# Two sides of memory, gate passes ahead of value passes, and the last GLA chain among the merge's first units, in a hybrid attention and GLA decoder step

## The chip, the core and the metric

The kernel runs on one core of one Trainium2 chip. A core has TensorE (PE, matrix multiply), VectorE (DVE), ScalarE (ACT), GpSimd (POOL) and SyncE (SP, which here issues nearly all DMA transfers), all started by their own streams of instructions and ordered among one another by semaphores. The metric is the device time of one execution in microseconds (us).

## What is computed

One decoder layer on 2048 prompt tokens and 8 x 8 sample tokens (2112 rows of 1024 numbers in float32). Cut to what matters:

```python
z = x @ w_in                      # q k v g_att gq gk gv g_gla g_lr r_att r_gla
o_att = sliding_window_attention(q, k, v)          # window 128, sinks, relative bias
o_gla, S = gated_linear_attention(gq, gk, gv, log_a)   # 4 heads, recurrent state S
h_att = (o_att * silu(g_att)) @ w_pa
h_gla = (norm(o_gla) * silu(g_gla)) @ w_pg
merged = sigmoid(r_att) * h_att + sigmoid(r_gla) * h_gla
x = layer_norm(alpha * x + merged @ w_o)
```

Every product of float32 matrices is done as three matmuls on split numbers: a tile is split into a high part (ScalarE, a cast) and a low part (VectorE, the difference), and hi x hi, hi x lo and lo x hi are added in PSUM. That is why each weight and each activation costs a cast on ACT and a subtraction on DVE (`split`, L113 to L115).

## The kernel before, in words

**Stages.** (1) Six chunks of 384, 384, 384, 384, 256 and 320 tokens go through attention (L520 to L622). (2) For each of four heads the same six chunks go through GLA (L832 to L919). (3) The merge multiplies four pairs of matrices (L929 to L1093). (4) The output stage multiplies by w_o and normalizes (L1099 to L1144). Results between the stages go through DRAM: `ua_d` (attention, gated), `ug_d` (GLA, gated), `mg_d` (merged).

**Ticks.** Inside stages 1 and 2 the big projections of a chunk are written in order, and after each stands a `tick()`. Small steps are put into a list by `at(d, fn)`, to be run at the d-th tick. In GLA the steps of a chunk (`gla_a`, `gla_b`, `gla_c`, for each block of 128 tokens, and for the last chunk of a head `samp_a`, `samp_b` for the sample tokens) thus run among the projections of the next chunk. `drain()` runs what is left. The last chunk of the last head has no next chunk: at L929 `drain()` runs its chain by itself, then the pool of buffers is closed and the merge's pool is opened.

For the last chunk of a head (two full blocks and 64 sample tokens) the ticks hold: `gla_a` of the blocks at 0 and 1, `samp_a` at 1 (it makes `kz` and loads two 512-KB state tiles, L779 to L782), `gla_b` of the blocks at 2 and 3, `samp_b(0)` at 3 right behind `gla_b` (its L795 reads both state tiles), `samp_b(4)` at 4. The next head's first chunk writes its first value tile before tick 0 and its second before tick 2.

**Order.** TensorE runs in the order in which the program is written. For the other engines and SP a planner fixes the order when the program is built, by its own estimate of when inputs and buffers are ready, with program order as the priority. On the chip each engine then keeps that order: an instruction that waits holds up those behind it, and so do DMA issues on SP.

**Buffers.** A pool has tags; tiles of a tag share a number of buffers. Tag `w` (28 tiles of 4 KB per partition) holds projection weights (high and low part), the operands of the combinations below, the sample caches kc and vc, and also scores, transposed scores, GLA's ring, states, values, kz and state tiles. A pool opened after another one closed reuses its memory, and each tile waits only for the tiles that lay where it lies.

**The merge.** Each of the four products (w_pa, w_ra, w_pg, w_rg; PA, RA, PG, RG below) is a `Pass` with Winograd's form of Strassen's seven products: `ORDER = (1, 2, 7, 6, 5, 3, 4)` are the operations, s = 0, 1, 2 are three strips of 704 tokens, each cut in two of 352. A unit is one operation on one strip, a group one of its four pairs of output blocks p (`for p in range(NP4)`). Before there are 4 x 7 x 3 = 84 units of 4 groups; a group is 12 matmuls (L1088 to L1090; 6 in PA). `combine` adds products into accumulators `ac` from PSUM; operations 2, 5, 3 and 4 each finish one output block, which goes to the pass's sink.

The passes run PA, RA, PG, RG. PA stores its result in `ha_d`. RA's sink (`sink_ra`, L1055) loads the partner from `ha_d`, takes tanh, forms (tanh + 1) * h (L1058) and stores `ta_d`. PG stores `hg_d`. RG's sink (`sink_rg`, L1061) loads two partners, from `hg_d` and `ta_d`, does the same (L1064), adds on POOL (L1065) and stores `mg_d`. A partner is loaded where the sink is written, with six buffers (tag `cs`).

The differences of the activations that the operations need are made beforehand for x and for the attention result (`combine_x`, L815: 18 combinations, each two loads, four POOL operations and four stores into `xc_d` or `ac_d`, in the first three chunks of heads 0, 1 and 2). For the GLA result (PG) they are made inside the pass on POOL (L1006) from two tiles, kept in `uc_d` and read again. x tiles are loaded one unit ahead (`mv`), weights three units ahead, all four p together (L1082), with differences on POOL (L962 to L973).

**The output stage.** After the merge's pool has closed, a new pool is opened; x tiles are read from `mg_d`, the eight tiles of w_o are loaded and split (through L127), then 17 blocks of rows run.

## Time and profile before

| | us |
|---|---|
| median of 3 runs | 1937.02 |
| lowest and highest run | 1935.22, 1937.87 |
| the profiled execution | 1931.98 |
| its span | 1930.2 |
| TensorE busy in it | 1821.2 (94%) |
| VectorE, ScalarE, POOL busy | 1234.5, 848.1, 504.7 |
| last matmul of GLA's last projection ends | 1078.1 |
| first matmul of the merge | 1103.09 |
| first matmul of the output stage | 1721.38 |

How to read it: the span runs from the first to the last instruction in the trace, and the execution is 1.8 us longer. Times are from the span's start. A row of a timeline has start, duration, engine, line, operation, tiles, and in brackets how long the engine sat idle before it and what ended that. In a row of windows the numbers are the window, its length, busy time and count for each engine (PE, PEld for weight loads, DVE, ACT, POOL; TensorE alone if one line is asked for), then the TensorE clock that was granted, as a share of full speed, the mean busy share of the 16 DMA engines, and GB/s. Matmuls overlap, so the duration of one is longer than the step from one to the next. L114 and L115 are `split`, whoever calls it.

### The profile page before, as it was taken

The numbers are of one execution on the slowest core, as the hardware profiler recorded it, in microseconds if no ns is written. First come the engines' busy times: TensorE is split into PE (matmuls) and PEld (weight loads), VectorE is DVE, ScalarE is ACT, GpSimd is POOL, SyncE is SP. The second block draws the span as 40 slices with busy tenths as digits, with TensorE's granted clock in tenths as the row PEclk, the third lists the DMA queues.
The fourth block names the chain that finished last, engine by engine and source line by source line (L and its number), as shares of the span: only waits on it lengthen the run. The fifth ranks groups of instructions, "written<-read, shape, count | busy, mean of one in ns | idle before, by whom it ended". The sixth has DMA issues, their size and how long they took to land.

```text
span 1930.2 us, 32049 instructions
## 1 busy us (share of the span) xinstructions
PE 1821.2 (94%) x11669; PEld 1728.9 (90%) x11669; DVE 1234.5 (64%) x2544; ACT 848.1 (44%) x1942; POOL 504.7 (26%) x632
## 2 busy tenths in 40 slices
PE   8799999899999999999999799999999989959997
PEld 7688998799999999999999699999989989847886
DVE  5386778655676676567565467678627566756565
ACT  4244446545665565566465343535423333331110
POOL 2410111412133114201101150420544354421121
PEclk9899999999999999999999899999999999969999
DMA  6411013543365246333221479769687765874432
GB/s 199 105 53 37 12 45 98 160 134 113 95 225 182 69 147 221 115 105 113 77 74 48 137 231 321 238 189 323 215 272 268 271 220 169 251 242 166 151 129 81
DMA packets 195038, 304.15 MB, mean 158 GB/s; under 512 B 20648, under 2 KB 162824, under 8 KB 194864
## 3 DMA queue, kind: packets, MB, share of 16 engines
q1 hardware_dynamic: 188960, 294.45, 46.8%
q0 software_dynamic: 5920, 7.66, 1.9%
q8 instruction: 91, 1.49, 0.3%
q14 instruction: 67, 0.55, 0.1%
HBM read 221.19 MB, written 81.81 MB: 157 GB/s over the span
## 4 chain that ended last, share of the span: by engine, by line
PE 72%; DMA 9%; POOL 6%; DVE 5%; issue 4%; ACT 2%; SPq 1%; POOLq 0%; DVEq 0%; ACTq 0%
PE pd L179 9%; PE pd L180 9%; PE pd L181 9%; PE pa L1089 6%; PE pa L1088 6%; PE pa L1090 6%; PE pd L194 6%; PE pd L193 6%; PE pd L192 6%; DMA bs_d<-brow 2%; DMA cs<-hg_d 2%; DMA xs<-ug_d 2%; PE pa L394 1%; DVE wl L115 1%; PE pa L379 1%
## 5 line engine op out<-in xcount | busy, mean ns | idle before, releaser
L179 PE MATMUL pd<-x,wh 128*128 128x384 f32 (+2 forms) x1248 | 409.9, 328 | 17.8 <-ACT x L114 17.1
L180 PE MATMUL pd<-x,wh 128*128 128x384 f32 (+2 forms) x1248 | 404.7, 324 | 3.9 <-DVE x L115 3.9
L181 PE MATMUL pd<-x,wl 128*128 128x384 f32 (+2 forms) x1248 | 404.1, 324 | 1.3 <-DVE wl L115 1.3
L1089 PE MATMUL pa<-xl,wh 128*128 128x352 f32 x1176 | 382.7, 325 | 16.9 <-DVE xl L115 16.5
L1088 PE MATMUL pa<-xh,wh 128*128 128x352 f32 x1176 | 384.2, 327 | 13.6 <-ACT xh L114 9.6
L1090 PE MATMUL pa<-xh,wl 128*128 128x352 f32 x1176 | 381.6, 324 | 0.0
L192 PE MATMUL pd<-wh,x 128*128 128x256 f32 (+1 forms) x768 | 251.6, 328 | 20.5 <-ACT wh L114 20.3
L179 PEld LDWEIGHTS pd<-x,wh 128*128 128x128 f32 x1248 | 237.1, 190 | 27.4 <-ACT x L114 17.7
L194 PE MATMUL pd<-wl,x 128*128 128x256 f32 (+1 forms) x768 | 248.3, 323 | 2.3 <-DVE wl L115 2.2
L193 PE MATMUL pd<-wh,x 128*128 128x256 f32 (+1 forms) x768 | 247.7, 322 | 0.4 <-POOL x L115 0.2
L1089 PEld LDWEIGHTS pa<-xl,wh 128*128 128x128 f32 x1176 | 224.7, 191 | 21.7 <-DVE xl L115 21.7
L180 PEld LDWEIGHTS pd<-x,wh 128*128 128x128 f32 x1248 | 237.2, 190 | 5.6 <-DVE x L115 5.6
L181 PEld LDWEIGHTS pd<-x,wl 128*128 128x128 f32 x1248 | 236.9, 190 | 1.9 <-DVE wl L115 1.9
L1088 PEld LDWEIGHTS pa<-xh,wh 128*128 128x128 f32 x1176 | 223.5, 190 | 16.4 <-ACT xh L114 10.3
L1090 PEld LDWEIGHTS pa<-xh,wl 128*128 128x128 f32 x1176 | 223.5, 190 | 0.0
L115 DVE TENSOR_TENSOR xl<-xs,xh 128x1408 fp32r<-128x1408 f32 (+1 forms) x84 | 130.5, 1553 | 123.2 <-ACT xh L114 108.5
L192 PEld LDWEIGHTS pd<-wh,x 128*128 128x128 f32 x768 | 148.5, 193 | 33.4 <-ACT wh L114 23.9
L114 ACT CAST xh<-xs 128x1408 fp32r<-128x1408 f32 (+1 forms) x84 | 102.8, 1224 | 143.5 <-PE pa L1090 84.1
L194 PEld LDWEIGHTS pd<-wl,x 128*128 128x128 f32 x768 | 148.1, 193 | 16.1 <-DVE wl L115 6.2
L193 PEld LDWEIGHTS pd<-wh,x 128*128 128x128 f32 x768 | 148.3, 193 | 10.8 <-POOL x L115 0.5
L114 ACT CAST x<-xst 128x384 fp32r<-128x384 f32 (+3 forms) x164 | 77.7, 485 | 146.4 <-PE pd L193 123.1
L712 POOL TENSOR_SCALAR sq<-sq 128x1 f32<-128x1 f32 (+1 forms) x68 | 18.8, 277 | 399.4 <-ACT ring L711 399.4
(288 smaller groups left out, 3233.1 us busy)
## 6 DMA issues: line engine op xcount, KB each, us to landing
wst<-wt SPq DMA_DIRECT2D x41, 512.0 KB, 3.6
xs<-ug_d SPq DMA_DIRECT2D x27, 704.0 KB, 6.2
xs<-xc_d SPq DMA_DIRECT2D x24, 704.0 KB, 6.1
u<-xT SPq DMA_DIRECT2D x84, 192.0 KB, 3.7
xst<-xT SPq DMA_DIRECT2D x76, 192.0 KB, 2.7
xs<-xT SPq DMA_DIRECT2D x18, 704.0 KB, 6.2
x<-xT SPq DMA_DIRECT2D x24, 352.0 KB, 5.7
xc_d<-x SPq DMA_DIRECT2D x48, 176.0 KB, 1.8
```

The source lines that it names most:

```text
L114: nc.scalar.copy(dst_h, src)
L115: eng.tensor_tensor(dst_l, src, dst_h.bitcast(F32), ALU.subtract)
L179: mm(ps, hi[:, s], xh[:, :T], start=(k == 0), stop=False)
L180: mm(ps, hi[:, s], xl[:, :T], start=False, stop=False)
L181: mm(ps, lo[:, s], xh[:, :T], start=False, stop=(k == n - 1))
L192: mm(ps, xh[:, xs], hi, start=(k == 0), stop=False)
L193: mm(ps, xl[:, xs], hi, start=False, stop=False)
L194: mm(ps, xh[:, xs], lo, start=False, stop=(k == KT - 1))
L379: nc.tensor.transpose(tp[:, g * P:(g + 1) * P], s[:, g, hf * W:(hf + 1) * W], ident)
L1088: mm(ps, wh[:, ks], xh[:, ts], start=(k == 0), stop=False)
L1089: mm(ps, wh[:, ks], xl[:, ts], start=False, stop=False)
L1090: mm(ps, wl[:, ks], xh[:, ts], start=False, stop=(k == q.kh - 1))
```

## The change

1. **Two sides.** The stages' memory is one pool on the left (`sb`) and one on the right (`sx`). Projection weights, x tiles, combination operands, kc, vc, kcT, vn and p12 go right: tag `xw` has 20 buffers. Scores, GLA's ring, states, values, kz and state tiles stay left: tag `w` has 8. The merge's tiles (`mb`) go right when `sx` closes, so the left pool can stay open for the last GLA chain.
2. **The last chain.** `drain()` no longer stands ahead of the merge. Units call `tick()` after every second group; at unit 6 what is left is drained, the left pool is closed, and pools for partners and `a21` (`ml`) and for combinations (`mc`) are opened there. Until then products use the three `pd` banks of PSUM, afterwards the five `pa` banks.
3. **Order of passes.** RA, PA, RG, PG. The gate passes store tanh in `ta_d` and `tg_d`; the value passes form (tanh + 1) * h, and PG adds `mg_d` of PA on POOL.
4. **U combinations.** Twelve more entries of `combine_x` make the four differences of the GLA result in units 8 to 52, one every four units; PG reads them like x.
5. **Fetching ahead.** x tiles are loaded two units ahead (three buffers) and split one ahead; weights are loaded one step and prepared one step ahead, p by p, spread over the three strips; operation 6 loads two of its blocks again and differences are formed in place. Partners are loaded four groups ahead (eight buffers).
6. **Output weights.** w_o has its own input; five of its eight tiles are loaded and split in units 64 to 80, the rest after the merge.

The diff, cut:

```diff
-        return sb.tile([P, D], dt, tag="w", name=name, bufs=28)
+        return sb.tile([P, D], dt, tag="w", name=name, bufs=8)
+
+    def xwtile(dt=F32, name="xw"):
+        return sx.tile([P, D], dt, tag="xw", name=name, bufs=20)
...
-        kc = wtile(name="kc").rearrange("p (b c) -> p b c", b=NB)
-        vc = wtile(name="vc").rearrange("p (b c) -> p b c", b=NB)
+        kc = xwtile(name="kc").rearrange("p (b c) -> p b c", b=NB)
+        vc = xwtile(name="vc").rearrange("p (b c) -> p b c", b=NB)
...
-                   [(io["xT"], xc_d, 4, k, s) for s in range(MS) for k in range(4)])
+                   [(io["xT"], xc_d, 4, k, s) for s in range(MS) for k in range(4)] +
+                   [(ug_d, uc_d, 4, k, s) for s in range(MS) for k in range(4)])
...
-    drain()
-    phase.close()
...
+    right.close()
+    mb = right.enter_context(tc.tile_pool(name="mb", bufs=1, side="right", reuse_waits="tile"))
...
+        def raw_w(self, i, p):
+            out = []
+            for c, k in {1: [(1, 1)], 2: [(1, 2)], 7: [(1, 1), (2, 1)], 6: [(2, 1), (2, 2), (1, 1)], 5: [],
+                         3: [(1, 2)], 4: [(2, 2)]}[i]:
+                t = mtile("ws", KT // 2 * P, 11)[:, :self.kh * P]
+                nc.sync.dma_start(t, self.w[c - 1, k - 1, p])
+                out.append(t)
+            return out
...
+        def partners(self, i, p, s):
+            if i not in FINAL:
+                return []
+            c, t = FINAL[i]
+            out = []
+            for d in self.parts:
+                y = ml.tile([P, T], F32, tag="cs", name="cs", bufs=8)
+                nc.sync.dma_start(y, d[:, 2 * p + c, toks(s, t)])
+                out.append(y)
+            return out
...
+    def gate_sink(dst):
+        def sink(z, parts, ct, ts):
+            nc.scalar.activation(z, z, AF.Tanh, scale=0.5)
+            nc.sync.dma_start(dst[:, ct, ts], z)
+        return sink
+
+    def merge_sink(z, parts, ct, ts):
+        nc.vector.scalar_tensor_tensor(z, parts[0], 1.0, z, ALU.add, ALU.mult)
+        if len(parts) > 1:
+            nc.gpsimd.tensor_tensor(z, z, parts[1], ALU.add)
+        nc.sync.dma_start(mg_d[:, ct, ts], z)
...
-    passes = [Pass(io["w_pa"], 2, ua_d, store_to(ha_d), ac_d, True),
-              Pass(io["w_ra"], 4, io["xT"], sink_ra, xc_d, True),
-              Pass(io["w_pg"], 4, ug_d, store_to(hg_d), uc_d, False),
-              Pass(io["w_rg"], 4, io["xT"], sink_rg, xc_d, True)]
+    passes = [Pass(io["w_ra"], 4, io["xT"], xc_d, [], gate_sink(ta_d)),
+              Pass(io["w_pa"], 2, ua_d, ac_d, [ta_d], merge_sink),
+              Pass(io["w_rg"], 4, io["xT"], xc_d, [], gate_sink(tg_d)),
+              Pass(io["w_pg"], 4, ug_d, uc_d, [tg_d, mg_d], merge_sink)]
...
     for n, (q, i, s) in enumerate(units):
-        xh, xl = mv
-        if n + 1 < len(units):
-            q2, i2, s2 = units[n + 1]
-            mv = q2.moving(i2, s2)
...
+        if n == 2 * MS:
+
+            drain()
+            left.close()
+            ml = left.enter_context(tc.tile_pool(name="ml", bufs=1, side="left", reuse_waits="tile"))
+            bg = ExitStack()
+            mc = bg.enter_context(tc.tile_pool(name="mc", bufs=1, side="left", reuse_waits="tile"))
+        if n == 3 * len(ORDER) * MS:
+            bg.close()
+            mo = left.enter_context(tc.tile_pool(name="mo", bufs=1, side="left", reuse_waits="tile"))
+        if ml is not None and n < 3 * len(ORDER) * MS and n % 4 == 0 and combos:
+            combine_x(lambda t: mc.tile([P, 2 * T], F32, tag="xc", name=t, bufs=4))
+        if mo is not None and n % 4 == 0 and len(wo) < 5:
+            wo.append(wo_load(mo, len(wo), 10))
+        issue_x(n + 2)
+        issue_w(n + 1)
+        make_x(n + 1)
+        make_w(n)
+        xh, xl = xp.pop(n)
         for p in range(NP4):
...
+            g = n * NP4 + p
+            if ml is not None:
+                for j in range(g, g + 4):
+                    if j not in parts:
+                        issue_parts(j)
...
+            q.combine(i, p, s, ps, parts.get(g))
+            if p % 2:
+                tick()
+    right.close()
```

More of the change, by code (lines that the diff above doesn't have):

```diff
@@ L848 @@
             gla_z(B)
-            if c < 3:
-                combine_x(2)
+            if c < 3 and len(combos) > 12:
+                for _ in range(2):
+                    combine_x(lambda n: xwtile(name=n))
             wv = [wt2("v", 0), wt2("v", 1)]
@@ L1072 @@
[L1072 to L1085 removed]
+                z = acc.pop((p, s, 12))
@@ new lines, in combine @@
+                add(z, z, ps, ALU.add)
+            else:
+                z = acc.pop((p, s, 21))
+                add(z, z, ps, ALU.subtract)
+            if z is not None:
+                c, t = FINAL[i]
+                self.sink(z, parts, 2 * p + c, toks(s, t))
+    def gate_sink(dst):
[8 more added lines that the diff above has]
+        nc.sync.dma_start(mg_d[:, ct, ts], z)
@@ new lines, with issue_w, make_w, issue_x @@
+    raws, wts, xs, xp, parts = {}, {}, {}, {}, {}
+    def issue_w(n):
+        for u, q, i, p in plan.get(n, []):
+            raws[u, p] = q.raw_w(i, p)
+    def make_w(n):
+        for u, q, i, p in plan.get(n, []):
+            wts[u, p] = q.prep_w(i, p, raws.pop((u, p)))
+    def issue_x(n):
+        if n < len(units):
+            q, i, s = units[n]
+            xs[n] = q.raw_x(i, s)
+    def make_x(n):
+        if n < len(units):
+            xp[n] = units[n][0].prep_x(xs.pop(n))
+    def issue_parts(g):
+        if g < len(groups):
+            q, i, s, p = groups[g]
+            parts[g] = q.partners(i, p, s)
@@ new lines, in wo_load @@
+    def wo_load(pool, i, bufs):
+        st = pool.tile([P, D], F32, tag="wst", name="wst", bufs=2)
+        nc.sync.dma_start(st, io["w_o"][i])
+        hi, lo = (pool.tile([P, D], F32R, tag="wo", name=n, bufs=bufs) for n in ("woh", "wol"))
+        split(hi, lo, st)
+        return hi, lo
+    issue_x(0)
+    issue_w(-1)
+    issue_x(1)
+    make_x(0)
+    make_w(-1)
+    issue_w(0)
+    ml = mc = mo = None
+    wo = []
+    for n, (q, i, s) in enumerate(units):
+        if n == 2 * MS:
[16 more added lines that the diff above has]
+        xh, xl = xp.pop(n)
+        for p in range(NP4):
+            g = n * NP4 + p
[3 more added lines that the diff above has]
+                        issue_parts(j)
+            wh, wl = wts[n - s, p]
+            ps = (pd() if ml is None else pa())[:, :T]
@@ L1144 @@
         x = xn
+    right.close()
+    left.close()
 def _consts():
@@ L1200, in _layout @@
         t += [cm(gg[:, h * HV + m * P:h * HV + (m + 1) * P]) for m in range(2)]
[L1201 to L1202 removed]
+    t_o = [rows(wo[:, nh * 512:(nh + 1) * 512], k0) for nh in range(2) for k0 in range(0, KT, 2)]
     def blocks(m):
```

228 lines of the change are left out of this document (80 added, 148 removed).

## The prediction

> **What bounds the kernel now.** I read the page first, then TensorE's waits and timeline, then counts of one matmul line over growing windows, which give the pace of each stage.
>
> ```profile
> span 1930.2 us, 32049 instructions
> PE 1821.2 (94%) x11669; PEld 1728.9 (90%) x11669; DVE 1234.5 (64%) x2544; ACT 848.1 (44%) x1942; POOL 504.7 (26%) x632
> ```
>
> TensorE carries the span, and the change takes no matmul away. So it can win only TensorE's holes, and lose by making new ones. The merge issues 1176 triples (L1088 to L1090). The next rows give window, length, busy time and, in brackets, how many L1090 had been issued by the window's end.
>
> ```profile
> 0.00:1110.00 1110.00, 3.29 (x8) 0.98 0.36 111
> 0.00:1190.00 1190.00, 54.66 (x168) 0.98 0.39 121
> 0.00:1350.00 1350.00, 161.76 (x503) 0.98 0.44 138
> 0.00:1525.00 1525.00, 272.46 (x844) 0.98 0.47 151
> 0.00:1705.00 1705.00, 381.60 (x1176) 0.98 0.50 159
> ```
>
> From 1190 to 1350 pass RA issued 335 triples in 160 us: 0.4776 us each, 7.63 us for a unit of 16. I take this as the full pace, since TensorE shows almost no wait there. PA (168 triples) would need 80.2 us at it, each other pass (336) 160.5. The holes are worst around the merge:
>
> ```profile
> 1077.81 0.31 PE L181 MATMUL pd<-x,wl 128*128 128x320 f32 x1
> 1078.00:1094.40 16.40, 11.26 (x72) 8.36 (x70) 9.90 (x36) 4.68 (x17) 3.52 (x6) 0.90 0.32 105
> 1103.09 0.66 PE L1088 MATMUL pa<-xh,wh 128*128 128x352 f32 x1 [8.76 <-ACT xh L114]
> 1721.38 0.80 PE L192 MATMUL pd<-wh,x 128*128 128x512 f32 x1 [17.09 <-ACT wh L114]
> 1760.00:1800.00 40.00, 40.00 (x178) 33.13 (x177) 25.43 (x37) 6.08 (x12) 6.75 (x8) 1.00 0.44 149
> 1700.00:1918.00 218.00, 102.21 (x256) 0.94 0.47 158
> 1916.95 0.28 PE L208 MATMUL pd<-wh,x 128*128 128x256 f32 x1
> ```
>
> The last projection ends at 1078.1, the last GLA chain runs alone (11.26 us busy of 16.4), and the merge starts at 1103.1: 25 us. With both tables PA took 87 us, RA 160.5, PG 172.5 (to 1523, its 840th triple), RG 181.3: the merge's last matmul ends at 1721.38 - 17.09 = 1704.3, and the output stage starts 17 us later. That stage's pace is 178 matmuls in 40 us, 0.2247 each; 256 triples (the count of L192) are 172.6 us, the 64 half-wide matmuls of the last block some 7.2, and 13.0 pass from the last matmul to the end: 193 us, against 225.9 since 1704.3.
>
> **The change part by part.**
>
> *Start of the merge.* The chain's ticks come every second group of the first units, whose inputs (xT, xc_d) don't wait for GLA. The chain keeps its TensorE work: 11.26 us at clock 0.90, say 10. The first unit still needs x and four weights split into tiles that GLA's last weights may hold; no row shows which. Bounds: 0, and 8.8 (today's wait). I take 3, because freed weight buffers let most loads go before 1078. VectorE and POOL take the chain's small steps between splits; the U differences start only at unit 8. So 25 becomes 13: **-12**.
>
> *Passes RA and RG (gates).* They lose the partner loads and the products. RA has no holes, so what is taken from it wins nothing: 160.5. RG becomes like RA: 161. Fetching two units ahead covers today's waits for x there.
>
> *Pass PA (value).* It gets what RA lost, in half the TensorE time: 48 partner loads and 48 products. VectorE first (count, busy us, mean ns):
>
> ```profile
> L115 DVE TENSOR_TENSOR xl<-xs,xh 128x704 fp32r<-128x704 f32 x21 | 20.8, 990 | 16.1 <-ACT xh L114 16.1
> L115 DVE TENSOR_TENSOR wl<-ws,wh 128x256 fp32r<-128x256 f32 x20 | 9.5, 513 | 0.9 <-ACT wh L114 0.9
> L1032 DVE TENSOR_TENSOR ac<-ac,pa 128x352 f32<-128x352 f32 x12 | 6.1, 511 | 0.0
> L1058 DVE SCALAR_TENSOR_TENSOR ac<-ac,cs 128x352 f32<-128x352 f32 x46 | 26.5, 586 | 4.8 <-ACT ac L1057 3.4 <-DMA cs<-ha_d 0.6
> ```
>
> 21 x 0.99 + 28 x 0.51 + 72 sums x 0.51 + 48 products x 0.59 = 100 us, above TensorE's 80. Now the bytes (KB each, us to landing):
>
> ```profile
> wst<-wt SPq DMA_DIRECT2D x41, 512.0 KB, 3.6
> xs<-xc_d SPq DMA_DIRECT2D x24, 704.0 KB, 6.1
> xc_d<-x SPq DMA_DIRECT2D x48, 176.0 KB, 1.8
> cs<-ha_d SPq DMA_DIRECT2D x48, 176.0 KB, 4.6
> x<-xT SPq DMA_DIRECT2D x24, 352.0 KB, 5.7
> ws<-w_pg SPq DMA_DIRECT2D x28, 256.0 KB, 4.3
> mg_d<-ac SPq DMA_DIRECT2D x48, 176.0 KB, 2.6
> ws<-w_pa SPq DMA_DIRECT2D x28, 128.0 KB, 3.5
> xs<-ua_d SPq DMA_DIRECT2D x9, 352.0 KB, 4.4
> 1160.00:1210.00 50.00, 49.04 (x303) 47.70 (x301) 37.41 (x67) 21.53 (x34) 3.92 (x3) 1.00 0.94 318
> 1630.00:1710.00 80.00, 67.92 (x396) 66.16 (x394) 55.78 (x89) 27.02 (x44) 36.08 (x34) 0.93 0.80 253
> ```
>
> In PA: 21 x tiles 7.6 MB, 36 weights 4.7 (28 before: operation 6 loads two blocks again), 48 partners and 48 stores 17.3, five U combinations (units 24 to 40) of two 352-KB loads and four 176-KB stores, 7.2, and 1.2 more for RG's larger first tiles: 38.0 MB. The last two rows end with the DMA share and GB/s: 318 at share 0.94 where PA and RA press the queues, 253 at 0.80 where RG loads two partners a group. 38.0 MB take 120 us at 318, 150 at 253. VectorE's 100 is the lower bound. I take 120, since partners now load four groups ahead and only bandwidth should hold them: **+33** on 87. The Trainium skill, "DMA: Bandwidth & Descriptors", section "Where 436 GB/s comes from", says that between HBM and SBUF the HBM side, about 358 GB/s per core, binds. By that figure PA would be an estimated 106 us and the sum 14 lower; the nearest row here shows 318, so I keep to that.
>
> *Pass PG.* POOL's in-line differences and the dependent reloads go, so U is read like x. But PG now takes RG's two partners. Its units that finish a block (operations 2, 5, 3, 4; FINAL) each move x 0.72 MB, 8 partners and 4 stores, 2.88 MB. The nine of 5, 3, 4 with weights 2.1 and two output weights 1.0, less 2.9 fetched ahead, need 26.3 MB; the three of 2 need 8.0. 34.3 MB at 318 are 108 us, the nine others 68.6 at TensorE's pace: 176.5. Bounds 160.5 and 204 (at 253). VectorE has RG's load of before. The four passes: 120 + 160.5 + 161 + 176 = 617.5 against 601.2: **+16**, PA's 33 included.
>
> *Output stage.* x of the first block depends on unit 81, two before the end, and five of eight output weights are split during PG (n = 64 to 80, behind its matmuls; uncovered, each would cost at least its landing of 3.6 us). Left: a short wait for x (3 us; bounds 0 and today's 17) and 2 for the last three weights. 198 for 225.9: **-28**.
>
> *Split of the weight buffers.* kc now shares a tag with projection weights and combinations, no longer with scores and GLA tiles.
>
> ```profile
> 368.65 8.70 SPq L830 DMA_DIRECT2D ac_d<-x  x8
> 377.44 0.38 SPq L408 DMA_DIRECT2D kc<-ck  x1
> 383.42 1.94 PE L416 MATMUL pa<-ident,kc 128*128 128x128 f32 x8 [8.56 <-DMA kc<-ck]
> ```
>
> Today SP issues kc behind stores that wait for POOL. With buffers free once the ga weights are used, kc can go before them: the 8.6 us hole closes, with about 3 us of slow restart (at 1103 the first row counts 8 triples in 6.9 us where 14.5 fit): **-11** (bounds 0, -12).
>
> The other side has eight buffers for GLA. At a head switch ring, st and ak hold three, the last chunk's values two, the next chunk's first value tile one, kz one, the first state tile one. The second state tile is the ninth.
>
> ```profile
> 563.25 2.63 SPq L781 DMA_DIRECT2D S<-state  x2
> 574.71 1.85 PE pa L795 x16
> L776 DVE TENSOR_TENSOR kz<-ss,bsel x4: 1217/1218/1222, 568.6 to 1082.4; 128x1024 fp32r<-128x1024 f32 x4
> DMA to landing us min/median/max: 4.0/5.7/7.0
> ```
>
> Today both state loads are issued by 565.9, 9 us before L795, which reads both. Now the second waits until gla_b of the last full block frees a value tile, and samp_b stands right behind that on TensorE. Nothing covers the landing (last row: state loads); every later projection waits on TensorE, and on SP the x loads of the next chunks queue behind the waiting load. 5.7 less 0.4 of matmuls in between, and 2 of slow restart (3 at most, as at 1103), make 7.3; three switches (the last head has no next chunk): **+22** (bounds 0 and 27). Zero holds if buffers aren't handed out in program order; the S loads stand beside kz in every head, so I lean to program order.
>
> Sum: -12 + 16 - 28 - 11 + 22 = -13, span 1917. The profiled execution took 1931.98, 1.8 over its span, and the median of the runs, 1937.02, is 5.0 above that: 1917 + 1.8 + 5.0 = **1924 us**. From no change this kernel's measurement can tell about 0.2%, 3.9 us.
>
> **The rivals.**
> - *Value passes at 253 GB/s* (slower). The row that shows two partners a group shows 253, not 318: partner buffers come free only after the products, so loads go out late however early they are written. For: that row's share of 0.80, not full. Against: today they are issued at the sink, with six buffers. PA 150, PG 204: 58 more, 1982. It decides below about 296 GB/s (72.3 MB of the bound parts then take 17 us more than at 318), where the time passes 1941.
> - *No wait at the head switches*: state loads get buffers before kz. 1924 - 22 = 1902.
> - *kc stays behind the combinations' stores*, as in today's SP order: 1935.
> - *The change doesn't hide the chain*: unit 0 stands ahead of the chain's first tick on TensorE; if its weights come only after 1078, with 704 KB and 4 x 256 KB to load, the chain waits behind them, some 12 us instead of 3: 1933.
>
> **How the numbers follow.** Forecast 0.42 (own range 1908 to 1941: PA 110 to 130, PG 168 to 185), slow value passes 0.17, no switch wait 0.21, kc 0.12, chain not hidden 0.08. Faster by over 0.2% (below 1933): 0.32 of the forecast, all of 0.21, 0.05 of kc, 0.03 of the last: 0.61. Slower (above 1941): 0.04 + 0.16 + 0.03 + 0.02 = 0.25. Within: 0.14. The range 1893 to 1960 reaches into both sides: below it the case without switch waits and with a lighter PA, above it most of the slow value passes.
>
> **What would show it.** Right: L1088 starts within 5 us of the last projection; PA takes 110 to 130 us with DMA share above 0.9; RG shows no wait above 1 us; L795 waits about 6 us for S in three places, and not at the last head; L416 has no wait; the output stage's first matmul comes within 6 us of the merge's last. Wrong: PA near 87 us, or partners landing late at a share below 0.85; L795 without a wait; a new hole in attention from its eight buffers.

## The result, and the profile after

The changed kernel takes **1986.04 us** (median of 4 runs, 1984.39 to 1990.4) against 1937.44 for the kernel before beside it (4 runs, 1935.22 to 1942.74): a ratio of 1.025, with a 95% interval of 1.0224 to 1.0277. The forecast was 1924, with a range up to 1960. The profiled execution is one of 1986.42 us.

The head of the page after:

```profile
span 1984.4 us, 32348 instructions
PE 1842.3 (93%) x11669; PEld 1738.6 (88%) x11669; DVE 1234.1 (62%) x2544; ACT 848.3 (43%) x1942; POOL 523.2 (26%) x668
```

The count of matmuls is what it was. The span is 54.2 us longer and TensorE's busy time 21.1 longer: besides new holes, there is work at a lower clock. Where it happens is read from stage marks. TensorE's timeline after has the gate matmul that opens each GLA head (L655; L652 before), the end of the last projection, and the first matmuls of the merge and of the output stage:

```profile
377.61 0.34 PE L655 MATMUL pd<-gin,wgk 96*128 96x384 f32 x1
581.29 0.67 PE L655 MATMUL pd<-gin,wgk 96*128 96x384 f32 x1
771.32 0.42 PE L655 MATMUL pd<-gin,wgk 96*128 96x384 f32 x1
957.01 0.42 PE L655 MATMUL pd<-gin,wgk 96*128 96x384 f32 x1
1135.68 0.31 PE L184 MATMUL pd<-x,wl 128*128 128x320 f32 x1
1142.99 0.66 PE L1126 MATMUL pd<-xh,wh 128*128 128x352 f32 x1 [6.56 <-ACT wh L117]
1778.56 0.80 PE L195 MATMUL pd<-woh,x 128*128 128x512 f32 x1 [6.96 <-ACT x L117]
```

The same marks before (the last projection, at 1078.1, is in the prediction):

```profile
364.19 0.34 PE L652 MATMUL pd<-gin,wgk 96*128 96x384 f32 x1
557.98 0.42 PE L652 MATMUL pd<-gin,wgk 96*128 96x384 f32 x1
732.58 0.42 PE L652 MATMUL pd<-gin,wgk 96*128 96x384 f32 x1
905.64 0.42 PE L652 MATMUL pd<-gin,wgk 96*128 96x384 f32 x1
```

The ends of the passes after come from the count of the third merge matmul (L1128) over growing windows, 336, 504, 840 and 1176 of them:

```profile
0.00:1325.00 1325.00, 109.52 (x336) 0.97 0.41 128
0.00:1442.00 1442.00, 165.89 (x504) 0.96 0.45 141
0.00:1608.00 1608.00, 274.45 (x840) 0.96 0.48 153
0.00:1772.00 1772.00, 382.88 (x1176) 0.97 0.51 161
```

| stage | before | after | difference | forecast |
|---|---|---|---|---|
| attention | 364.2 | 377.6 | +13.4 | 0 |
| GLA head 0 | 193.8 | 203.7 | +9.9 | -11 |
| head 1 | 174.6 | 190.0 | +15.4 | +7 |
| head 2 | 173.1 | 185.7 | +12.6 | +7 |
| head 3 | 172.5 | 179.0 | +6.5 | +7 |
| last projection to last merge matmul | 626.2 | 635.6 | +9.4 | +4 |
| output stage | 225.9 | 212.8 | -13.1 | -28 |

All of the loss, 58 us, is made before the merge begins. Three places show how. First, attention. TensorE has one long hole there; VectorE stood at a score that waited for its bias (L360), with the gate's product (L218), which TensorE needed, queued behind it. The timeline after, lines of GpSimd, VectorE and TensorE in order of time:

```profile
79.87 4.33 POOL L297 DMA_DIRECT2D bias<-bs_d  x8 [35.02 <-DMA bs_d<-brow]
...
82.90 0.42 DVE L360 TENSOR_TENSOR s<-pa,bias 128x256 f32<-128x256 f32 x1 [36.35 <-DMA bias<-bs_d]
...
85.00 0.55 DVE L218 SCALAR_TENSOR_TENSOR sil<-th,pd 128x384 f32<-128x384 f32 x1
...
85.61 0.69 PE L182 MATMUL pd<-x,wh 128*128 128x384 f32 x1 [27.05 <-DVE sil L218]
```

Before, the bias was issued earlier, the gate's product stood ahead of the score, and TensorE's holes were 11 and 3 us:

```profile
71.60 4.33 POOL L294 DMA_DIRECT2D bias<-bs_d  x8 [33.68 <-DMA bs_d<-brow]
...
72.41 0.69 PE L179 MATMUL pd<-x,wh 128*128 128x384 f32 x1 [11.23 <-ACT x L114]
...
78.26 0.69 PE L180 MATMUL pd<-x,wh 128*128 128x384 f32 x1 [2.97 <-DVE x L115]
```

Second and third, the switch of heads. The table of waits after (total, times, longest) has the state wait that was forecast, and two that were not: GpSimd at a combination's sum that waits for its load, and TensorE at the transpose of GLA's normed output (`ring`).

```profile
PE pa L798 <- DMA S<-state: 14.6, 3, 5.9
PE pa L750 <- ACT ring L717: 11.4, 7, 5.0
POOL x L826 <- DMA x<-xT: 34.7, 9, 7.5
```

Before, the last two were

```profile
PE pa L747 <- ACT ring L714: 5.9, 8, 1.7
POOL x L825 <- DMA x<-xT: 1.3, 2, 0.8
```

One such spot in the timeline after, at the first switch. On GpSimd the norm's two small operations (L715, L716) stand behind half a combination, which waits 4.55 us for its load. Then, on TensorE, the transpose that needed the norm, and later the state wait:

```profile
577.62 0.92 POOL L826 TENSOR_TENSOR x<-x,x 128x352 f32<-128x352 f32 x1 [4.55 <-DMA x<-xT]
578.62 0.93 POOL L827 TENSOR_TENSOR x<-x 128x352 f32<-128x352 f32 x1
579.51 0.22 POOL L715 TENSOR_SCALAR sq<-sq 128x1 f32<-128x1 f32 x1
579.82 0.57 POOL L716 TENSOR_TENSOR sq<-sq,mhalf 128x1 f32<-128x1 f32 x1
...
580.95 0.69 PE L750 MATMUL pa<-ident,ring 128*128 128x128 f32 x2 [5.01 <-ACT ring L717]
...
605.67 3.62 PE L798 MATMUL pa<-S,qz 128*32 128x256 f32 x14 [5.94 <-DMA S<-state]
```

The window behind the state's hole (the last three numbers are granted clock, DMA share, GB/s):

```profile
605.00:615.00 10.00, 9.33 (x44) 7.04 (x45) 4.52 (x6) 0.00 (x0) 6.03 (x7) 0.69 0.63 211
```

The clock is 0.69 there over 9.33 us of work: this hole costs about 3 us more than its length. In head 0 the norm is not the only small step that stands among sums: TensorE also waits 2.58 and 1.52 us (at 383 and 386) for x tiles that GpSimd splits among the sums of a combination.

The sync queue shows why that load was late: the second load of the combination stands behind the four stores of the one before it, and those wait for its sums. The second state is issued 9.6 us after the first, behind four stores more:

```profile
571.04 2.37 SPq L831 DMA_DIRECT2D xc_d<-x  x4
573.47 0.44 SPq L824 DMA_DIRECT2D x<-xT  x1
...
590.78 0.43 SPq L784 DMA_DIRECT2D S<-state  x1
...
596.80 3.01 SPq L831 DMA_DIRECT2D xc_d<-x  x4
...
600.38 0.40 SPq L784 DMA_DIRECT2D S<-state  x1
```

### The profile page after: what moved, and what is told of

It is laid out like the page before. It is cut to its first block, busy times and chain, and to the rows that moved or that the text cites. A ratio compares the mean times of both kernels' runs of the same rounds, so it can differ in the third digit from the quotient of the medians.

```text
span 1984.4 us, 32348 instructions
## 1 busy us (share of the span) xinstructions
PE 1842.3 (93%) x11669; PEld 1738.6 (88%) x11669; DVE 1234.1 (62%) x2544; ACT 848.3 (43%) x1942; POOL 523.2 (26%) x668
## 4 chain that ended last, share of the span: by engine, by line
PE 57%; DMA 8%; DVE 4%; POOL 4%; issue 2%; ACT 1%; SPq 1%; POOLq 0%; DVEq 0%; ACTq 0%
PE pa L1127 6%; PE pa L1126 6%; PE pa L1128 6%; PE pd L196 6%; PE pd L197 5%; PE pd L195 5%; PE pd L182 5%; PE pd L183 5%; PE pd L184 5%; DMA cs<-tg_d 2%; DMA x<-xT 1%; PE pa L722 1%; PE pa L724 1%; PE pa L723 1%; DVE xl L118 1%
## 5 line engine op out<-in xcount | busy, mean ns | idle before, releaser
L1126 PE MATMUL pa<-xh,wh 128*128 128x352 f32 x1080 | 355.2, 329 | 23.2 <-DVE a L1022 8.5
L1127 PE MATMUL pa<-xl,wh 128*128 128x352 f32 x1080 | 352.8, 327 | 11.9 <-DVE xl L118 11.9
L1128 PE MATMUL pa<-xh,wl 128*128 128x352 f32 x1080 | 351.2, 325 | 0.0
L1126 PEld LDWEIGHTS pa<-xh,wh 128*128 128x128 f32 x1080 | 206.2, 191 | 28.9 <-DVE a L1022 10.9
L1127 PEld LDWEIGHTS pa<-xl,wh 128*128 128x128 f32 x1080 | 207.3, 192 | 16.0 <-DVE xl L118 15.9
L1128 PEld LDWEIGHTS pa<-xh,wl 128*128 128x128 f32 x1080 | 206.5, 191 | 0.0
L196 PE MATMUL pd<-wh,x 128*128 128x256 f32 x512 | 149.6, 292 | 8.2 <-POOL x L118 4.1
L195 PE MATMUL pd<-wh,x 128*128 128x256 f32 x512 | 150.9, 295 | 3.9 <-DVE sg L218 3.9
L197 PE MATMUL pd<-wl,x 128*128 128x256 f32 x512 | 147.1, 287 | 0.0
L715 POOL TENSOR_SCALAR sq<-sq 128x1 f32<-128x1 f32 (+1 forms) x68 | 17.0, 250 | 406.2 <-ACT ring L714 406.2
L196 PEld LDWEIGHTS pd<-wh,x 128*128 128x128 f32 x512 | 100.4, 196 | 12.0 <-DVE x L118 7.0
L195 PE MATMUL pd<-woh,x 128*128 128x512 f32 x256 | 102.6, 401 | 8.0 <-ACT x L117 8.0
L366 ACT ACTIVATE s<-s,nm 128x256 f32<-128x256 f32 (+1 forms) x128 | 62.7, 491 | 107.2 <-DVE nm L364 105.9
```

What stands on the lines that cost most here:

```text
L195: mm(ps, xh[:, xs], hi, start=(k == 0), stop=False)
L196: mm(ps, xl[:, xs], hi, start=False, stop=False)
L197: mm(ps, xh[:, xs], lo, start=False, stop=(k == KT - 1))
L366: nc.scalar.activation(s[:, g, k0:], s[:, g, k0:], AF.Exp, bias=nm[:, g:g + 1], accum_out=sm[:, g:g + 1])
L1126: mm(ps, wh[:, ks], xh[:, ts], start=(k == 0), stop=False)
L1127: mm(ps, wh[:, ks], xl[:, ts], start=False, stop=False)
```

## The experiments

The theory (T1): the loss is the split of memory, by the order and the buffers of the combinations and by the hole in attention, with the state waits beside them. The rival (T2): the new merge carries it. Each was timed beside the kernel before on its own chip (medians of it 1933.2 to 1934.2). Ends of the last projection, which close the part before the merge:

| kernel | span | last projection ends | median, ratio to before (95%) |
|---|---|---|---|
| before | 1930.2 | 1078.1 | |
| after | 1984.4 | 1136.0 | 1986.04, 1.025 (1.0224 to 1.0277) |
| e1_split | 1985.9 | 1134.2 | 1988.03, 1.0281 (1.0255 to 1.0307) |
| e2_merge | 1928.2 | 1079.4 | 1931.75, 0.9991 (0.9975 to 1.0007) |
| e3_state | 1982.8 | 1131.6 | 1982.39, 1.0254 (1.022 to 1.0289) |
| e4_combos | 1970.7 | 1121.1 | 1973.15, 1.0209 (1.018 to 1.0239) |
| e5_nosum | 1946.5 | 1099.4 | 1950.81, 1.0091 (1.0075 to 1.0107) |
| e6_lag | 1968.8 | 1120.6 | 1973.25, 1.0216 (1.0191 to 1.0242) |
| e8_three | 1933.8 | 1085.0 | 1935.32, 1.0001 (0.9983 to 1.0018) |
| e10_stores | 1996.3 | 1149.9 | 1998.75, 1.0329 (1.0312 to 1.0346) |
| e13_late | 1991.9 | 1141.0 | 1993.17, 1.0289 (1.0264 to 1.0314) |
| e14_all | 1965.5 | 1111.6 | 1962.27, 1.0146 (1.013 to 1.0162) |
| e7_order | 1933.2 | | 1935.85, 1.0011 (0.9998 to 1.0023) |
| e11_uc | 1932.4 | | 1930.5, 0.9977 (0.9964 to 0.999) |
| e12_prod | 1966.0 | | 1966.07, 1.0162 (1.0141 to 1.0183) |
| e9_both | 1967.0 | | 1973.53, 1.0195 (1.0173 to 1.0217) |
| e15_sigm | 1942.2 | | 1940.26, 1.0032 (1.0019 to 1.0044) |

**Which half.** The split alone, in the kernel before:

```diff
-    sb = phase.enter_context(tc.tile_pool(name="sb", bufs=1, reuse_waits="tile"))
+    sb = phase.enter_context(tc.tile_pool(name="sb", bufs=1, side="left", reuse_waits="tile"))
+    sx = phase.enter_context(tc.tile_pool(name="sx", bufs=1, side="right", reuse_waits="tile"))
...
-        return sb.tile([P, D], dt, tag="w", name=name, bufs=28)
+        return sb.tile([P, D], dt, tag="w", name=name, bufs=8 if sx is not sb else 28)
+    def xwtile(dt=F32, name="xw"):
+        return sx.tile([P, D], dt, tag="xw", name=name, bufs=20)
```

> The kernel before with nothing of the change but the two memory parts in attention and the GLA (8 weight-sized buffers on the left, 20 on the right, stages, x and weight stages on the right); its own merge and output stage, which begin after the whole GLA. Theory T1 (the split of memory carries the loss: attention +13, the four heads +10, +15, +13, +7): span near 1930 + 58 = 1988, with the hole of some 27 us in attention and the three waits for a state at the switch of heads in it. Rival T2 (the new merge carries it, the split costs only what was forecast, 22 for the states less 11 for kc): span near 1941. Third theory T3 (neither alone: the split hurts only because 12 more combinations and the chain's ticks are in the program behind it): near 1950, and no hole in attention.

And the new merge and output stage alone, behind one memory:

```diff
-        return sb.tile([P, D], dt, tag="w", name=name, bufs=8)
+        return sb.tile([P, D], dt, tag="w", name=name, bufs=28)
...
-    right.close()
+    drain()
+    left.close()
```

> The changed kernel's merge and output stage (gate passes first, tiles two units ahead, w_o early) behind the kernel before's attention and GLA in one memory of 28 weight-sized buffers; the last GLA chain is drained before the merge, as before. T1: the GLA ends where it did before (last projection 1078), the merge starts 25 us later as before, and merge and output take what they took after the change, 841 us from the first merge matmul to the end of the span, less the GLA chain's 10 us and perhaps less the hole of 11: 1103 + 820 to 831 = span 1923 to 1934. T2: the loss comes with the merge, span 1975 or more.

Spans of 1985.9 and 1928.2: T1 on both; T2 and T3, the third theory of the first text, fall. The split alone ends its last projection 56 us later than before, with the hole in attention (25.7 us) and the three state waits in it. The new merge with one memory is no different from the kernel before within what can be measured.

**The state tiles.** In the changed kernel:

```diff
-            S0 = wtile(name="S0").rearrange("p (b v) -> p b v", b=4)
+            S0 = (wtile if B["h"] == GH - 1 else xwtile)(name="S0").rearrange("p (b v) -> p b v", b=4)
```

> The changed kernel with the two state tiles of each of the first three heads taken from the right part's 20 buffers in place of the left part's 8. T1a (the second state's late buffer is the cost of the heads): the three waits of a matmul for a state, 14.6 us, go, and with them some of the slow clock behind each: span 1962 to 1970. T1b (the cost of the heads is the order in which the planner put the combinations ahead of the GLA's own work on GpSimd and the sync queue): the three waits go or are put in place of by others at the same spots, and the span falls by less than 8. T2: no change.

The three state waits are gone and the span is 1.6 shorter, so T1a does not hold by itself; T1b, by which other waits take their place, fits. At the switch to head 3, around which no combinations stand, head 3 returns to 172.4 us (172.5 before). At the switches to heads 1 and 2 the wait moved to another norm (2.66 and 2.22 us, for the sample tokens' ring), and heads 1 and 2 stay at 192 and 187.

**The combinations.** First written some 20 us later in the program:

```diff
             gla_z(B)
-            if c < 3 and len(combos) > 12:
-                for _ in range(2):
-                    combine_x(lambda n: xwtile(name=n))
...
             gla_q(B, ps[:, :T])
             tick()
+            if c < 3 and len(combos) > 12:
+                for _ in range(2):
+                    combine_x(lambda n: xwtile(name=n))
```

> The changed kernel with each chunk's two combinations written some 20 us later in the program, behind the k and q projections in place of behind the gate's projection; the same work and the same buffers. T1b (combinations that the planner puts ahead of the norm on GpSimd hold up the GLA at each switch of heads): the waits of the transposed norm for the scaled ring (11.4 us in three places) go and the heads are shorter, span 1960 to 1972. T1a: the span stays within 5 of 1984, since the state waits stand. T2: no change.

The span, 1970.7, is T1b's, but its mechanism came true in part only. The last projection ends 14.9 us earlier, 9.9 of them in head 0 (193.8). At the first two switches the ring waits (3.85 and 4.37 us) and the state waits stand as they stood without the edit, and head 0 has a new ring wait of 3.06 us. In the trace GpSimd's order at the first switch is the same one, half a combination, a norm, and the next combinations: the place in the program did not set it.

Then without their arithmetic on GpSimd:

```diff
-        nc.gpsimd.tensor_tensor(x2[:, t1], x2[:, t1], x1[:, t1], ALU.subtract)
+        if src is ug_d:
+            nc.gpsimd.tensor_tensor(x2[:, t1], x2[:, t1], x1[:, t1], ALU.subtract)
...
```

> The changed kernel without the four sums on GpSimd of each combination in the GLA (18 combinations, 72 sums; their loads and stores stay, so what is stored is not combined: the merge's operands are wrong, its work is the same). T1b (GpSimd runs in order and stands at a sum that waits for its load, and the norm behind it waits): the waits of a matmul for the scaled ring, 11.4 us in three places, go, heads 0 to 2 get shorter, and the span falls by 15 to 25, to 1960 to 1970; the three waits for a state stand. T1c (the loads and stores of the combinations in the sync queue and on the DMA engines are what delays): the ring waits may go, but others come at the same places and the span stays above 1976. In both, attention keeps its hole and head 3 its 179.

Two rows of its table of waits:

```profile
PE pa L798 <- DMA S<-state: 12.9, 3, 5.3
PE pa L750 <- ACT ring L717: 2.7, 7, 0.5
```

The heads' first matmuls in the timeline of e5_nosum (the first head starts at 375.28):

```profile
559.45 0.42 PE L655 MATMUL pd<-gin,wgk 96*128 96x384 f32 x1
740.38 0.42 PE L655 MATMUL pd<-gin,wgk 96*128 96x384 f32 x1
920.58 0.42 PE L655 MATMUL pd<-gin,wgk 96*128 96x384 f32 x1
```

T1b, and more than it expected: the span falls by 37.9. The ring waits are down to 2.7 us, the state waits stand. The four heads take 184.2, 180.9, 180.2 and 178.9 us, against 203.7, 190.0, 185.7 and 179.0 with the sums. So the sums cost 34 us of the heads. TensorE's idle time in heads 0 to 2 falls from 37.1 to 16.3 us, 8.7 of it at the norm (11.4 to 2.7); the other 13 us are lower clock (0.96 over head 0 with the sums, 1.00 without). The run doesn't tell the sums from the stores that wait for them. What is left against the kernel before is -9.6 in head 0, where the hole at `kc` is closed, and +6.3, +7.1 and +6.4 in the others, where the state waits stand.

**The hole in attention.**

```diff
-        lag = 2 if c == 0 else 0
+        lag = 4 if c == 0 else 0
```

> The changed kernel with the first chunk's scores two steps later in the program (a lag of 4 in place of 2). T1 (attention's 13 us are one hole, in which VectorE stands at the first score, which waits for its bias, ahead of the gate's product that TensorE waits for): the hole of 27 us shrinks to the 14 of before or less, the stage up to the first GLA matmul falls from 377.6 to about 364, and the span to about 1971. Rival (the hole is the wait for the bias row's 33 us write, which fills the DMA engines, and moving the scores only changes who waits): the hole stays above 22 us and the span within 6 of 1984.

T1: attention ends at 367.5, and its holes are again the two of before (10.41 and 4.24 us, behind x). The span is 15.6 shorter. Of attention's 13.4 us, 3.3 stay.

**All three together.** The edits of e3, e5 and e6:

> The changed kernel with three edits together: the state tiles of the first three heads from the right part, the sums of the 18 combinations in the GLA left out (the merge's operands are then wrong, its work the same), and the first chunk's scores two steps later. If hole, sums and states are all that the split of memory costs, the stages up to the last projection take what they took before (1078 in place of 1136) and the span is 1922 to 1935. If something else of the split costs too (the loads and stores of the combinations, or buffers for weights), it stays above 1945.

The first outcome: the span is 1933.8, and the last projection ends at 1085.0, so 51 of the 58 us are accounted for. Of the 7 that stay, 3.6 are in attention (367.8); heads 1 and 2 are 5.6 and 7.5 longer than before, and head 0 is 9.8 shorter by `kc`. In heads 1 and 2 a wait for x (2.33 and 2.42 us, each with 0.93 more behind it) stands where the state wait was, so without the state waits these heads take what they took with them (180.2 and 180.6, against 180.9 and 180.2 in e5_nosum). Head 3 alone gets its time back, 172.4.

**Is it the queue, the place or the work?** The stores moved from the sync queue to GpSimd:

```diff
-            nc.sync.dma_start(dst[n_, :, s, k], x_[:, t])
+            (nc.sync if src is ug_d else nc.gpsimd).dma_start(dst[n_, :, s, k], x_[:, t])
```

> The changed kernel with the four stores of each combination in the GLA issued by GpSimd, behind its sums, in place of the sync queue. If the coupling of the two queues is what delays (a load and the second state stand in the sync queue behind four stores that wait for the sums, and the sums wait for the load): the three state waits (14.6 us) go, the waits for the scaled ring shrink below 6 us, and the span falls to 1955 to 1970. If it is only GpSimd's own order (a sum that waits for its load ahead of a norm): the ring waits stay, GpSimd has 72 more DMA issues of some 0.6 us in front of the norms, and the span is 1980 to 1995.

From its table of waits:

```profile
POOL x L826 <- DMA x<-xT: 5.8, 2, 3.0
PE pa L750 <- ACT ring L717: 16.0, 7, 7.0
```

The second outcome, at 1996.3 just above its range. GpSimd now hardly waits for loads, so the coupling with the sync queue is undone, and yet the norms come later than ever: from 565 to 607 us GpSimd works through six combinations of four sums and four issues, with two norms among them. The state waits stand (4.88, 4.55 and 3.17 us), so the stores ahead of the load don't make them. This fits a cost of whatever stands ahead of the norm on GpSimd, whether it works or waits; but the 72 issues are new work there, so the run alone doesn't prove it. Writing the combinations in the last three chunks of a head:

```diff
-            if c < 3 and len(combos) > 12:
+            if c >= 3 and len(combos) > 12:
```

> The changed kernel with the combinations of the first three heads written in the last three chunks of each head in place of the first three (same work, same buffers). On GpSimd the program's order is then: of the six that stood around each switch of heads, two go ahead of the last chunk but one, and the rest follow one chunk at a time. If it is the crowding at the switch that costs (sums behind loads, the second state behind stores, just where the norms come every 10 us), the waits for the scaled ring and the states shrink and the span falls to 1945 to 1965. If a combination costs the same wherever it stands, the holes move with them and the span stays within 10 of 1984.

The second outcome. The ring waits only moved (4.13 us in head 0, then 5.28, 5.03 and 4.97 at the switches), and the switch to head 3, which had none, got one. With the edits of e3_state and e6_lag beside this one:

> The changed kernel with three edits that keep all of its work: combinations in the last three chunks of a head, state tiles of the first three heads from the right part, and the first chunk's scores two steps later. If placement is the whole loss, it comes to what the run without the sums came to, 1934, or with the hidden chain a little below, 1922 to 1940. If the split has a cost that no placement takes away, it stays above 1950.

This keeps all work. Attention (367.0) and the state waits are mended, the ring waits stay, one of 4.4 us in head 0 and one of 5.1 to 5.7 at each switch, and at 1962.27 it is above 1950, the second outcome: none of the three places that these runs used carries the combinations without loss in the split memory. Why the planner puts them differently with 20 buffers on the right than with 28 shared is not shown by any run, and no run changes the two counts, so the sides and the counts are not told apart either.

**The value pass.** Since the merge alone gains nothing, the question is where its gains went. The passes in the old order, with its sinks:

```diff
-    passes = [Pass(io["w_ra"], 4, io["xT"], xc_d, [], gate_sink(ta_d)),
-              Pass(io["w_pa"], 2, ua_d, ac_d, [ta_d], merge_sink),
+    passes = [Pass(io["w_pa"], 2, ua_d, ac_d, [], store_sink(ha_d)),
+              Pass(io["w_ra"], 4, io["xT"], xc_d, [ha_d], gate_sink(ta_d)),
...
-        if n >= 2 * MS and n < 3 * len(ORDER) * MS and n % 4 == 0 and combos:
+        if n >= 7 * MS and n % 2 == 1 and combos:
```

> The first form with the new merge and one memory (1931.75 in the runs) with the passes in the order of the kernel before: values ahead of gates, so that the partners are loaded in the gate passes; the prefetch, the early w_o and the combined inputs of the second value pass stay. As forecast for the attention value pass (its loads and stores at the bandwidth and its work on VectorE set its length, 118 us measured against 87 before): it falls to 85 to 95, the gate passes take 165 to 175, the span falls by 15 to 30, to 1898 to 1913. Rival (the pass is long for another reason, such as the fewer buffers of finished tiles): it stays above 105 us, and the span stays above 1920.

PA falls from 109 us (e2_merge; the texts below put it at 113) to 88, as expected, but the span, 1933.2, is the rival's. RA, which now has the partners and eight of the twelve late combinations' sums, rises from 171 to 191, PG from 164 to 176: moved, not saved. Then edits of PA on top of e2_merge (e9_both has the first two and eight buffers of finished tiles):

```diff
# e11_uc
+        if combos and (2 * MS <= n < 7 * MS and n % 4 == 0 or 14 * MS <= n < 21 * MS and n % 2 == 0):
# e12_prod, in merge_sink for PA
+            nc.gpsimd.tensor_scalar(parts[0], parts[0], 1.0, None, op0=ALU.add)
+            nc.gpsimd.tensor_tensor(z, z, parts[0], ALU.mult)
# e15_sigm (with e11_uc): gates by AF.Sigmoid, and
+        (nc.vector if len(parts) > 1 else nc.gpsimd).tensor_tensor(z, z, parts[0], ALU.mult)
```

> One memory and the new merge with only the second value pass's combinations moved out of the first value pass (4 in the first gate pass, 8 in the second). The five moved are some 7 MB of loads and stores, 22 us at the 320 GB/s of that pass. If the DMA engines set the pass: 113 falls to 90 to 95 and the span to 1908 to 1916. If VectorE sets it (busy all of the time in its last 40 us): it falls by less than 8 and the span stays above 1923.

> One memory and the new merge with only the product of the first value pass on GpSimd. If VectorE sets the pass: its last 40 us, in which VectorE had no gap and GpSimd nothing to do, shorten by 10 to 20, and the span is 1912 to 1922. If the DMA engines set it: VectorE gets gaps, the pass stays at 110 or more and the span above 1926.

> One memory and the new merge (1931.75 in the runs) with three edits in the merge: the second value pass's combinations are taken out of the first value pass (4 in the first gate pass, 8 in the second), the product of that value pass goes to GpSimd (an addition of 1 and a multiplication there, in place of one operation on VectorE), and 8 buffers of finished tiles in place of 6. If bandwidth and VectorE set that pass's 113 us, as the traces read, it falls to 85 to 95, the first gate pass loses the stop of 4.4 us, and the span is 1895 to 1912, which beats both kernels. If the time only moves on, as it did with the passes in the old order, the passes' sum stays within 8 of 610 and the span above 1920.

> One memory and the new merge with the second value pass's combinations out of the first value pass (1930.5 in the runs), and the gate written as a sigmoid, which is half of 1 + tanh(z/2), so that the first value pass's product is one multiplication on GpSimd (0.94 us each, 48 of them, 45 us in a pass of 113 in which GpSimd worked 31) and not an operation on VectorE; the factor 2 is left out of the residual and of the norm's epsilon. If VectorE sets that pass and GpSimd holds out (76 us of 113), it falls to 95 to 105 and the span to 1912 to 1922. If GpSimd's operations, at twice VectorE's time, become the chain of the finished tiles, as in the run with two operations (141 us), it is 1930 or more.

PA took 113 us in e11_uc, 133 in e12_prod, 141 in e9_both and 121 in e15_sigm, against 109 in e2_merge. None of these runs settles what sets it.

e11_uc doesn't test the DMA engines, because on the chip its edit moved nothing. The stores of the combinations that fall into PA, e2_merge (PA from 1276 to 1385) and then e11_uc (count, ns of an issue, first and last issue):

```profile
L831 SPq DMA_DIRECT2D uc_d<-x x8: 319/424/624, 1285.0 to 1298.4; - x8
L831 SPq DMA_DIRECT2D uc_d<-x x9: 320/426/643, 1275.4 to 1300.4; - x9
```

Where the program has five combinations in PA, the traces of both kernels have ten of the twelve ahead of PA and the last two in its first 25 us: the planner had moved them already. Both move about the same bytes in PA: 293 GB/s over 109 us and 292 over 113, 32 and 33 MB. e12_prod and e9_both take the product off VectorE, but as two operations on GpSimd, which is then busy 110 of PA's 133 us in e12_prod: they show a new limit and not the old one. In e9_both neither outcome came: the passes' sum is 648 and not near 610. e15_sigm is the second outcome of its text, with products of 1.05 and 1.19 us on GpSimd where 0.94 was expected. A stretch of 25 us in PA, e11_uc and then e15_sigm (the third group is VectorE, the fifth GpSimd):

```profile
1350.00:1375.00 25.00, 20.69 (x106) 16.73 (x106) 25.00 (x56) 7.80 (x13) 0.00 (x0) 1.00 0.97 314
```

```profile
1350.00:1375.00 25.00, 21.51 (x121) 19.26 (x122) 24.77 (x44) 7.14 (x13) 20.49 (x20) 1.00 0.87 280
```

VectorE is full in both, with 56 operations and with 44, so part of what was taken off it came back as slower operations (below). But in e11_uc the DMA engines are at a share of 0.97 in the same stretch, and in PA's first 25 us VectorE is busy 8.5 us only, while TensorE waits for x. VectorE in the second half, bandwidth, and the landing of x at the start all remain possible. e11_uc at 0.9977 is the one version a little ahead of the kernel before, at the edge of what can be measured and not told apart from e2_merge.

## Why the prediction was wrong

- **The step that failed is "Split of the weight buffers".** It counted the left part's eight buffers and `kc`, and noted that `kc` shares its tag "with projection weights and combinations", but gave the combinations themselves no price. Where 0 was written, their sums cost 34 us (e5_nosum) and attention's hole 13 (10 of it by e6_lag). The kernel before and e2_merge do the same sums in their heads without this loss, so it is their place among GpSimd's steps that costs, and not their work. The prediction named "a new hole in attention from its eight buffers" only as a sign of error; the runs show the hole, but as an order on VectorE, not as a wait for one of the eight.
- **What it did price there had the right size.** State waits: forecast 7.3 each, three times; measured 6.3, 7.1 and 6.4 (e5_nosum, with 12.9 us of waiting), in heads 1 to 3 and not at the last end. That the state alone makes them is shown for head 3; in heads 1 and 2 a wait for x took its place (e8_three). `kc`: forecast -11, measured -9.6.
- **Start of the merge**: 7.0 us after the last projection against 3 plus 10 for the chain. The forecast's reason, that most loads go before the projection ends, is wrong: the first four weights are issued behind two stores at 1138.67, and the first matmul waits 6.56 us for them.

```profile
1137.54 1.07 SPq L757 DMA_DIRECT2D ug_d<-sg  x2
1138.67 1.86 SPq L958 DMA_DIRECT2D ws<-w_ra  x4
```

  The chain then runs among RA's units, where its matmuls still need TensorE: RA takes 182 us. Of those 8.0 are a hole (below) and some 3 its slow clock (0.68 from 1274 to 1284); the other 171 are RA's 160.5 and the chain's 10, as forecast.
- **Passes.** PA 117 (forecast 120), RG 166 (161), PG 164 (176.5). PA's size came out by luck: the forecast has 38.0 MB at 318 GB/s, the trace 286 GB/s over 117 us, which is 33.5 MB. Whether bytes set it is open. PG's bound by bytes did not hold: it took 13 us less, with no wait of TensorE above 1.5 us.
- **A term left out in RA.** VectorE waits 15 us for one of six buffers of finished tiles whose store hasn't landed, and TensorE 8 (the rows below). Eight buffers did not help where this was run: e9_both has 4.52 us there, e2_merge 4.37.

```profile
1273.35 0.52 DVE L1021 TENSOR_TENSOR fin<-a,pa 128x352 f32<-128x352 f32 x1 [15.19 <-DMA ta_d<-fin]
1274.36 0.66 PE L1126 MATMUL pa<-xh,wh 128*128 128x352 f32 x1 [8.00 <-DVE a L1022]
```

- **Output stage**: -13 against -28. The wait for x is 7.0 and not 3; the 11.5 us behind it run at a clock of 0.70, some 3 us; and the pace is 0.2312 us a matmul against 0.2247 (173 in 40 us against 178), 5 us over 768 matmuls. The last is not explained by any run.
- **The rivals.** The one on the slower side gave 1982 and was near the time by accident: its mechanism, PA and PG at 253 GB/s, did not happen (PA and PG took 281 together, not 354). "No switch wait" and "`kc` stays" are refuted. Of "the change doesn't hide the chain" the mechanism came true, since the chain waits behind the first unit's late weights; its size did not, with 7.0 us and not 12.

## What to carry to other kernels

When one pool of buffers is cut in two, list every tag that moves, and for each the engine queues its instructions stand in: here the order of the in-order engines changed with the split, and the price was paid by whoever stood behind. Price the small operations of the critical chain on the engine that also does bulk work (here a norm of 0.8 us behind sums of 0.9 us each and their loads): they need that engine to be free at the right moment, which no busy share shows. Work that is moved from one pass to the next is only gained if the receiving pass has room for it: in e7_order PA lost 21 us and RA gained 20. And before a run is read as a test, look in its trace whether the edit moved the work at all: in e11_uc it did not.

## What the runs showed of the hardware that was not expected

- VectorE slows when GpSimd works beside it. In PA GpSimd is busy 31 of 113 us in e11_uc and 78 of 121 in e15_sigm. VectorE's split of an x tile in PA (two inputs in SBUF) took 959 ns in e11_uc and 1259 in e15_sigm, the 128x256 splits of weights 587 and 712; additions of PSUM to a tile took 506 and 510. Rows of VectorE's groups, e11_uc and then e15_sigm (count, busy us, mean ns):

```profile
L118 DVE TENSOR_TENSOR xl<-xs,xh 128x704 fp32r<-128x704 f32 x21 | 20.1, 959 | 25.6 <-ACT xh L117 25.5
L1022 DVE TENSOR_TENSOR fin<-a,pa 128x352 f32<-128x352 f32 x12 | 6.1, 506 | 0.0
```

```profile
L118 DVE TENSOR_TENSOR xl<-xs,xh 128x704 fp32r<-128x704 f32 x21 | 26.4, 1259 | 24.8 <-ACT xh L117 24.8
L1022 DVE TENSOR_TENSOR fin<-a,pa 128x352 f32<-128x352 f32 x12 | 6.1, 510 | 0.2 <-DMA mg_d<-fin 0.2
```

  The Trainium skill, "GPSIMD Engine Reference", section "Specifications", says that GpSimd's access to SBUF is shared with VectorE and contends with VectorE's instructions that have two SBUF inputs. The rows agree, in which operations slow and in which don't.
- Idle time need not be in one piece for a lower clock. In e8_three TensorE waits 2.33 us until 590.56 and 0.93 until 591.88, with 0.4 us of matmuls between, and the granted clock of the 10 us from 590 is 0.66. The Trainium skill, "TensorE: Matmul & The Clock Gate", section "What's actually happening", has the clock fall after an idle window of about 3.4 us; here the longer of the two waits is 2.33 us, and the two together are 3.26.
